# Moving the modulation's vector products behind late tiles, output weights and evacuations

## Chip, cores and metric

One core of a Trainium2 chip runs one launch of the kernel. The metric is device time in microseconds (us), the median of three runs. The engines are TensorE (PE, matrix products), VectorE (DVE), ScalarE (ACT), GpSimd (POOL, idle here) and SyncE (SP), which issues every DMA. Each takes its instructions in a fixed order, and waits by semaphores for the others.

## What is computed

One layer of a streaming encoder, in float32, for 1024 tokens of width 1024, cut to what matters here:

```python
mod = silu(c) @ ada_w + ada_b                     # 6 x 1024 values
shift1, scale1, gate1, shift2, scale2, gate2 = split(mod, 6)
h = rmsnorm(x, norm1_g) * (1 + scale1) + shift1
u_lx, u_ly, u_b, u_c, u_v = split(h @ w_in)       # 5 x 512 columns
y_lru = headwise_rmsnorm(gelu(u_ly) * rg_lru(conv4(u_lx)))
y_conv = headwise_rmsnorm(u_b * conv3(u_c * u_v))
x = x + gate1 * (concat(y_lru, y_conv) @ w_out)
h2 = rmsnorm(x, norm2_g) * (1 + scale2) + shift2
x = x + gate2 * (square(relu(h2 @ w_mlp1)) @ w_mlp2)
return rmsnorm(x, final_g)
```

## The kernel before

Activations lie transposed: 128 features on the partitions, tokens along the row, in two chunks of 512 tokens (`cc` 0 and 1), eight blocks of features (`n` or `k`). Every float32 operand of a large product is split into a high and a low part of type float32r (`split`, L98: an ACT copy L100, then a DVE subtraction L101), and a product is three matmuls (`mm3`, lines L105, L107, L109). The MLP behind it, from about 350 us on, uses seven products of half-size blocks in place of eight; the change does not touch it.

The order on each engine comes from a scheduler that places the program's instructions by their operands and its own estimates of time. Only `after(inst, prev)` adds an order by hand: `inst` is put behind `prev` on an engine, without a semaphore.

The stages around the change:

- Twenty column tiles of `w_in` (`nt`): 0 to 3 feed the recurrence, 4 to 7 its gelu, 8 to 19 the short convolution (b, c, v). Seven (`START`) come first, then thirteen (`LATE`, index `i` 0 to 12), whose weights are loaded and split by `load_late`. Each tile ends in a PSUM bank that `evac` empties by ACT and DVE.
- When a recurrent tile `n` has both parts, `lru_c(n)` runs the gates: two small products on PE, sigmoid, tanh, exp and square root on ACT, and on DVE the steps L450, L456, the scan L458 and L459, which multiplies by the gelu. `conv_v` and `conv_b` do the same for the convolution (L477, L481). Then `norm_out` squares, splits and sums over heads with two statistics matmuls by the block matrix `bones` (L409 with the high part, L410 with the low), and scales.
- `w_out` comes in eight blocks (`load_w(OS[n], wout[n])`). The output projection writes banks 0 to 5, then 0, 1, 2 again; `evac_out` (L571) empties a bank: L573 multiplies by gate1 and adds x, a DMA writes x to `x1d`, ACT squares (L575), L577 adds the squares. When all eight blocks of a chunk are in, `norm2` sums them over partitions with the row-sum matmul L703.

The modulation for the first norm is made early. The other 32 rows of `ada_w` (16 to 47, gate1 first, then scale2 and shift2 in turn, then gate2) are made by **vector products**: `gemv(idx)` (L207) loads 128 x 1024 of `ada_w` by SP into one of two buffers that `vraw` hands out in turn, and one DVE instruction, L210, multiplies it by silu(c) and sums along the row into a column of `mods`; one or two scalar instructions (L215, L216, L219) turn the column into the value used. `more_gemv(n)` (L223) takes the next n of the rows 16 to 39. Before, it is called once in each late tile but the first, twice among the output weights, and for the rest at the evacuations of chunk 0; the only order by hand is that a product comes behind `h_done`, the end of the first norm of chunk 1. So the scheduler may take a product as soon as its data is there.

Of the kernel before, what the change touches and what calls it, by code (L numbers as in the profile page):

```python
# [12 lines left out]
ALU = mybir.AluOpType  # L13
# [4 lines left out]
H = 512  # L18
# [17 lines left out]
def block_kernel(ctx, tc, xT, vec, adaT, winA, winB, gw, wout, w1, w2, outT):  # L36
# [5 lines left out]
    def sb(name, shape, dt=F32):  # L42
        return pool.tile(shape, dt, name=name, tag=name)
# [10 lines left out]
    G = sb("G", [P, 2, H])  # L54
# [14 lines left out]
    A, V, T, dma = nc.scalar.activation, nc.vector, nc.tensor, nc.sync.dma_start  # L69
# [5 lines left out]
    def fl(ap):  # L75
        return ap.rearrange("p a b -> p (a b)")
# [12 lines left out]
    def vraw():  # L89

        vraw_i[0] += 1
        return (raws[2], F[:, 16:18, :])[vraw_i[0] % 2]

    def kc(k):

        return slice(k % 4 * P, k % 4 * P + P)
# [15 lines left out]
    def rs_(i):  # L112
        return R[:, i, HI, :], R[:, i, LO, :]
# [14 lines left out]
    def after(inst, prev):  # L128

        tc.add_manual_dep(ins_of(inst), ins_of(prev).name, NOSYNC, reason="order")  # L130
        return inst
# [75 lines left out]
    def gemv(idx, r=None, cv=None):  # L207
        r = vraw() if r is None else r
        after(dma(r, adaT[idx].rearrange("p (a b) -> p a b", b=H)), last)
        g = V.scalar_tensor_tensor(fl(r), fl(r), 0.5, fl(cb) if cv is None else cv, op0=ALU.mult, op1=ALU.mult, accum_out=mods[:, idx : idx + 1])  # L210
        after(g, h_done)

    def mod_scale_shift(base, k, gcol):
        i = base + 2 * k
        V.tensor_scalar(md[:, i : i + 1], mods[:, i : i + 1], pre[:, i : i + 1], gcol, op0=ALU.add, op1=ALU.mult)  # L215
        V.tensor_scalar(md[:, i + 1 : i + 2], mods[:, i + 1 : i + 2], vt[:, V_ADAB + i + 1 : V_ADAB + i + 2], None, op0=ALU.add)  # L216

    def mod_gate(i):
        V.tensor_scalar(md[:, i : i + 1], mods[:, i : i + 1], vt[:, V_ADAB + i : V_ADAB + i + 1], None, op0=ALU.add)  # L219
# [3 lines left out]
    def more_gemv(n):  # L223
        for _ in range(n):
            if gq:
                i = gq.pop(0)
                gemv(i)
                if i < 24:
                    mod_gate(i)
                elif i % 2 == 1:  # L230
                    k = (i - 25) // 2
                    mod_scale_shift(24, k, vt[:, V_N2 + k : V_N2 + k + 1])
# [32 lines left out]
    with tc.manual_schedule(engines={ET.DVE, ET.Activation, ET.SP}):  # L265
# [9 lines left out]
        for k in range(KT):  # L275
            i = T.matmul(banks[k // 4][:, kc(k)], lhsT=sc[:, k : k + 1].broadcast_to([P, P]), rhs=ident, start=True, stop=True)
# [41 lines left out]
        for k in range(KT):  # L318
# [32 lines left out]
            for j in range(NS):  # L351
                i = mm3([(banks[j],) + rs_(2 * k)], *wk(16 + 2 * j, k), k == 0, k == KT - 1)
# [81 lines left out]
    def lru_c(n):  # L434
        for cc in range(NCH):
            XL, G, r, I, TN, M = lset(cc)
            ba, bx = aux(), aux()
            xp = rs_(16 + 2 * n + cc)
            split(xp, XL)
            mm3([(ba,) + xp], gwh[:, 0, n, :], gwl[:, 0, n, :], True, True)  # L440
            mm3([(bx,) + xp], gwh[:, 1, n, :], gwl[:, 1, n, :], True, True)
            TA(r, ba, AF.Sigmoid, bias=vt[:, V_GAB + n : V_GAB + n + 1])
            TA(I, bx, AF.Sigmoid, bias=vt[:, V_GXB + n : V_GXB + n + 1])
            V.tensor_tensor(I, I, XL, op=ALU.mult)
        for cc in range(NCH):
            XL, G, r, I, TN, M = lset(cc)
            TA(TN, r, AF.Tanh, scale=sp8[:, n : n + 1])
            TA(r, r, AF.Exp, scale=nsp8[:, n : n + 1])
            A(M, r, AF.Square)
            V.scalar_tensor_tensor(M, M, 1.0, TN, op0=ALU.add, op1=ALU.mult)  # L450
        for cc in range(NCH):
            XL, G, r, I, TN, M = lset(cc)
            TA(M, M, AF.Sqrt)
            if cc == 0:
                V.memset(M[:, 0:1], 1.0)
            V.tensor_tensor(I, I, M, op=ALU.mult)  # L456
            init = 0.0 if cc == 0 else lset(cc - 1)[4][:, H - 1 : H]
            V.tensor_tensor_scan(TN, r, I, init, op0=ALU.mult, op1=ALU.add)  # L458
            V.tensor_tensor(G, G, TN, op=ALU.mult)  # L459
            later.append(lambda cc=cc, G=G, M=M, I=I: norm_out(n, cc, G, M, I, aux(), n))  # L460

    def conv_c(n, cc, pc):
# [2 lines left out]
    def conv_v(n, cc, pv):  # L465
        CV, CC = E[:, 2 + cc, :], cset(cc)[0]
        w = lambda j: vt[:, V_SCW + 3 * n + j : V_SCW + 3 * n + j + 1]
        if cc == 0:
            V.memset(CV[:, 0:2], 0.0)
        else:  # L470
            V.tensor_copy(CV[:, 0:2], vh[:, n, :])
        V.tensor_tensor(CV[:, 2 : H + 2], pv, CC, op=ALU.mult)
        if cc + 1 < NCH:
            V.tensor_copy(vh[:, n, :], CV[:, H : H + 2])
        A(CC, CV[:, 2 : H + 2], AF.Identity, scale=w(2))
        for j in range(2):
            V.scalar_tensor_tensor(CC, CV[:, j : j + H], w(j), CC, op0=ALU.mult, op1=ALU.add)  # L477

    def conv_b(n, cc, pb):
        CV, (CC, SQ) = E[:, 2 + cc, :H], cset(cc)  # L480
        V.tensor_tensor(CC, CC, pb, op=ALU.mult)  # L481
        later.append(lambda: norm_out(4 + n, cc, CC, SQ, CV, aux(), 4 + n))

    def evac(nt, cc, bank):
# [19 lines left out]
    def load_w(slot, src):  # L504
        r = raw()
        dma(r, src.rearrange("p (a b) -> p a b", b=H))
        return split((R[:, slot : slot + 2, HI, :], R[:, slot : slot + 2, LO, :]), r)
# [37 lines left out]
    for i, nt in enumerate(LATE):  # L545
        load_late(i + 3)
        b0, b1 = bank(), bank()
        for k in range(KT):
            mm3([(b0,) + rs_(2 * k), (b1,) + rs_(2 * k + 1)], *wk(ring[i % 4], k), k == 0, k == KT - 1)
        evac(nt, 0, b0)  # L550
        evac(nt, 1, b1)
        if nt // 4 == 1:
            lru_c(nt % 4)
        flush()
        more_gemv(1 if i else 0)


    OS = [32, 34, 36, 0, 2, 4, 6, 8]
    for q in range(4):
        load_x(0, q)  # L560
    for n in range(KT):
        load_w(OS[n], wout[n])
        more_gemv(n % 4 // 3)

    def gate(base, n):
        return md[:, base + n : base + n + 1]
# [3 lines left out]

    def evac_out(n, cc, b, first, acc, sqt, cs=slice(0, H), add=True):  # L571
        x, acc, sqt = x1(cc, n)[:, cs], acc[:, cs], sqt[:, cs]
        V.scalar_tensor_tensor(x, b, gate(16, n), x, op0=ALU.mult, op1=ALU.add)  # L573
        dma(x1d[cc, :, n, cs], x)
        A(acc if first else sqt, x, AF.Square)  # L575
        if add and not first:
            V.tensor_tensor(acc, acc, sqt, op=ALU.add)  # L577
# [13 lines left out]
    for n in (6, 7):  # L591
        for k in range(KT):
            mm3([(banks[n - 6],) + y_(k, 0)], *wk(OS[n], k), k == 0, k == KT - 1)
        evac_out(n, 0, banks[n - 6], False, e4[0], e4[2 + n % 2])
        more_gemv(2)
    for q in range(4):
        load_x(1, q)
    more_gemv(48)
# [400 lines left out]
    for u in range(8, 16):  # L999
        v = u - 8  # L1000
        g, half = v // 2, v % 2
# [160 lines left out]
```

## Time and profile before

| | |
|---|---|
| median of 3 runs | 984.37 us (983.35 to 984.83) |
| profiled execution | 982.71 us |
| its span, first to last instruction | 980.8 us |
| PE busy | 963.6 us, 98%, granted clock 0.998 |
| DVE busy | 750.2 us, 76% |
| ACT busy | 536.2 us, 55% |
| DMA | 154.50 MB, 158 GB/s on average |

A profile shows one execution. Busy time of PE is modelled: a matmul that follows a wait is drawn longer, and one is drawn until it leaves the array, while the next has begun. Idle time before an instruction is shown in brackets with what ended it.

### The profile page before, as it was taken

How to read it: one execution, taken by the hardware profiler on the slowest of the kernel's cores; microseconds unless marked ns; L12 is line 12 of the kernel's file. 1: busy time of each engine (PE TensorE's matmuls, PEld its weight loads, DVE VectorE, ACT ScalarE, POOL GpSimd, SP SyncE). 2: the span in 40 equal slices, each digit the busy share in tenths (PEclk: the TensorE clock that was granted, in tenths of full speed). 3: DMA queues.
4: the chain of work that ended last, by engine and by line, in shares of the span. 5: the costliest groups of instructions: out<-in, count | busy, mean ns of one | idle time of the engine just before them, and what ended most of it. 6: DMA issues, size and time to landing. Idle time of an engine off the chain costs nothing.

```text
span 980.8 us, 11613 instructions
## 1 busy us (share of the span) xinstructions
PE 963.6 (98%) x4430; PEld 797.7 (81%) x4430; DVE 750.2 (76%) x1001; ACT 536.2 (55%) x719; POOL 0.2 (0%) x4
## 2 busy tenths in 40 slices
PE   8999999999999999999999999999999999999996
PEld 6878778777888998888888888887888888888885
DVE  7989999967445889876655555798599599589657
ACT  6778888775322577554454554683253243144444
POOL 0000000000000000000000000000000000000000
PEclk9999999999999999999999999999999999999999
DMA  8925245234132131765533525789456157144005
GB/s 312 346 101 181 91 138 196 99 109 172 65 108 97 49 114 57 263 233 187 182 130 127 215 93 188 255 274 348 151 171 216 65 168 239 65 150 172 1 1 171
DMA packets 53287, 154.50 MB, mean 158 GB/s; under 512 B 5104, under 2 KB 10736, under 8 KB 53232
## 3 DMA queue, kind: packets, MB, share of 16 engines
q1 hardware_dynamic: 53232, 153.77, 44.7%
q8 instruction: 34, 0.56, 0.2%
q14 instruction: 21, 0.17, 0.1%
HBM read 116.00 MB, written 37.75 MB: 157 GB/s over the span
## 4 chain that ended last, share of the span: by engine, by line
PE 82%; DVE 9%; ACT 4%; DMA 3%; issue 2%; DVEq 0%; SPq 0%; ACTq 0%
PE bank L105 27%; PE bank L109 27%; PE bank L107 27%; DVE R L101 2%; DMA F<-adaT 2%; DVE F L427 1%; ACT F L400 1%; DVE F L210 1%; DVE F L458 1%; ACT R L100 1%; DMA gh<-hidd 1%; ACT L400 1%; DMA E<-hidd 1%; DVE F L459 0%; PE bank L410 0%
## 5 line engine op out<-in xcount | busy, mean ns | idle before, releaser
L105 PE MATMUL bank<-R 128*128 128x512 f32 (+1 forms) x1416 | 521.5, 380 | 3.8 <-DVE lp L182 2.0
L107 PE MATMUL bank<-R 128*128 128x512 f32 (+1 forms) x1416 | 520.7, 379 | 0.0
L109 PE MATMUL bank<-R 128*128 128x512 f32 (+1 forms) x1416 | 517.6, 379 | 0.0
L105 PEld LDWEIGHTS bank<-R 128*128 128x128 f32 x1416 | 266.4, 188 | 57.0 <-ACT R L241 3.0
L109 PEld LDWEIGHTS bank<-R 128*128 128x128 f32 x1416 | 266.2, 188 | 50.5 <-DVE R L245 0.4
L107 PEld LDWEIGHTS bank<-R 128*128 128x128 f32 x1416 | 266.4, 188 | 49.8 <-issue 0.7
L100 ACT ACTIVATE R<-F 128x1024 fp32r<-128x1024 f32 (+1 forms) x175 | 165.6, 958 | 178.5 <-PE bank L109 118.9
L101 DVE TENSOR_TENSOR R<-F,R 128x1024 fp32r<-128x1024 f32 (+1 forms) x175 | 190.1, 1097 | 58.9 <-ACT R L100 58.6
L986 DVE SCALAR_TENSOR_TENSOR F<-bank,md,F 128x512 f32<-128x512 f32 (+1 forms) x120 | 84.8, 711 | 48.8 <-PE bank L109 47.7
L899 ACT ACTIVATE F<-bank 128x512 f32<-128x512 f32 x44 | 26.2, 596 | 48.8 <-PE bank L109 48.4
L100 ACT ACTIVATE R<-G 128x1024 fp32r<-128x1024 f32 x23 | 24.3, 1057 | 32.6 <-PE bank L109 22.1
L101 DVE TENSOR_TENSOR R<-G,R 128x1024 fp32r<-128x1024 f32 x23 | 28.1, 1220 | 13.3 <-ACT R L100 13.3
L100 ACT ACTIVATE R<-E 128x1024 fp32r<-128x1024 f32 x26 | 27.4, 1054 | 8.9 <-DMA E<-hidd 8.6
L101 DVE TENSOR_TENSOR R<-E,R 128x1024 fp32r<-128x1024 f32 x26 | 31.6, 1217 | 0.0
L210 DVE SCALAR_TENSOR_TENSOR F<-F 128x1024 f32<-128x1024 f32 x24 | 29.0, 1216 | 1.7 <-DMA F<-adaT 1.6
L575 ACT ACTIVATE E<-F 128x512 f32<-128x512 f32 (+1 forms) x21 | 11.1, 528 | 32.2 <-DVE F L573 30.2
L400 ACT ACT_TABLE_LOAD x22 | 28.2, 1283 | 0.4
L899 ACT ACTIVATE E<-bank 128x512 f32<-128x512 f32 x20 | 11.9, 595 | 23.4 <-PE bank L109 23.4
L573 DVE SCALAR_TENSOR_TENSOR F<-bank,md,F 128x512 f32<-128x512 f32 (+1 forms) x21 | 12.7, 620 | 15.5 <-PE bank L109 15.5
L914 ACT ACTIVATE F<-bank 128x512 f32<-128x512 f32 x16 | 9.5, 597 | 20.3 <-PE bank L109 19.0
L903 ACT ACTIVATE F<-F 128x1024 f32<-128x1024 f32 x18 | 18.9, 1050 | 2.8 <-DVE F L933 1.5
L904 ACT ACTIVATE F<-F 128x1024 f32<-128x1024 f32 x18 | 19.1, 1058 | 0.4
(198 smaller groups left out, 734.8 us busy)
## 6 DMA issues: line engine op xcount, KB each, us to landing
F<-w SPq DMA_DIRECT2D x51, 512.0 KB, 3.8
hidd<-F SPq DMA_DIRECT2D x47, 512.0 KB, 4.5
F<-adaT SPq DMA_DIRECT2D x44, 512.0 KB, 4.3
E<-hidd SPq DMA_DIRECT2D x26, 512.0 KB, 5.5
F<-xT SPq DMA_DIRECT2D x16, 512.0 KB, 5.8
F<-hidd SPq DMA_DIRECT2D x15, 512.0 KB, 4.8
gh<-hidd SPq DMA_DIRECT2D x15, 512.0 KB, 5.1
F<-winB SPq DMA_DIRECT2D x13, 512.0 KB, 3.3
```

The lines of the kernel that those rows point to most:

```text
L100: a = A(dst[0], src, AF.Copy)
L101: return a, V.tensor_tensor(dst[1], src, fp(dst[0]), op=ALU.subtract)
L105: i = [T.matmul(b, lhsT=wl, rhs=xh, start=start, stop=False, **kw) for b, xh, xl in outs]
L107: T.matmul(b, lhsT=wh, rhs=xh, start=False, stop=False, **kw)
L109: T.matmul(b, lhsT=wh, rhs=xl, start=False, stop=stop, **kw)
L210: g = V.scalar_tensor_tensor(fl(r), fl(r), 0.5, fl(cb) if cv is None else cv, op0=ALU.mult, op1=ALU.mult, accum_out=mods[:, idx : idx + 1])
L400: i = A(*args, **kw)
L573: V.scalar_tensor_tensor(x, b, gate(16, n), x, op0=ALU.mult, op1=ALU.add)
L899: A(t[:, q, :], bk2[q], AF.Copy)
L903: A(t, t, AF.Relu)
L904: A(t, t, AF.Square)
L986: done_by["bank"] = V.scalar_tensor_tensor(x1(cc, n)[:, cs], b, gate(40, n), x1(cc, n)[:, cs], op0=ALU.mult, op1=ALU.add)
```

## The change

A list `near` collects DVE instructions as the program is written out: the steps of a recurrent or convolution tile, the low split of a `wout` block, and the evacuation L573. A vector product is put behind the newest of them. `more_gemv` now takes none in the late tiles 0 to 7, two in each of 8 to 12, one behind each of the `wout` blocks 3 to 7, and one behind each evacuation of chunk 0; the rest (one) comes after.

```diff
--- before.py
+++ after.py
@@ -209,6 +209,11 @@
         after(dma(r, adaT[idx].rearrange("p (a b) -> p a b", b=H)), last)
         g = V.scalar_tensor_tensor(fl(r), fl(r), 0.5, fl(cb) if cv is None else cv, op0=ALU.mult, op1=ALU.mult, accum_out=mods[:, idx : idx + 1])
         after(g, h_done)
+        if near:
+            after(g, near[-1])
+
+
+    near = []
 
     def mod_scale_shift(base, k, gcol):
         i = base + 2 * k
@@ -456,7 +461,7 @@
             V.tensor_tensor(I, I, M, op=ALU.mult)
             init = 0.0 if cc == 0 else lset(cc - 1)[4][:, H - 1 : H]
             V.tensor_tensor_scan(TN, r, I, init, op0=ALU.mult, op1=ALU.add)
-            V.tensor_tensor(G, G, TN, op=ALU.mult)
+            near.append(V.tensor_tensor(G, G, TN, op=ALU.mult))
             later.append(lambda cc=cc, G=G, M=M, I=I: norm_out(n, cc, G, M, I, aux(), n))
 
     def conv_c(n, cc, pc):
@@ -474,11 +479,11 @@
             V.tensor_copy(vh[:, n, :], CV[:, H : H + 2])
         A(CC, CV[:, 2 : H + 2], AF.Identity, scale=w(2))
         for j in range(2):
-            V.scalar_tensor_tensor(CC, CV[:, j : j + H], w(j), CC, op0=ALU.mult, op1=ALU.add)
+            near.append(V.scalar_tensor_tensor(CC, CV[:, j : j + H], w(j), CC, op0=ALU.mult, op1=ALU.add))
 
     def conv_b(n, cc, pb):
         CV, (CC, SQ) = E[:, 2 + cc, :H], cset(cc)
-        V.tensor_tensor(CC, CC, pb, op=ALU.mult)
+        near.append(V.tensor_tensor(CC, CC, pb, op=ALU.mult))
         later.append(lambda: norm_out(4 + n, cc, CC, SQ, CV, aux(), 4 + n))
 
     def evac(nt, cc, bank):
@@ -552,15 +557,15 @@
         if nt // 4 == 1:
             lru_c(nt % 4)
         flush()
-        more_gemv(1 if i else 0)
+        more_gemv(2 if i > 7 else 0)
 
 
     OS = [32, 34, 36, 0, 2, 4, 6, 8]
     for q in range(4):
         load_x(0, q)
     for n in range(KT):
-        load_w(OS[n], wout[n])
-        more_gemv(n % 4 // 3)
+        near.append(load_w(OS[n], wout[n])[1])
+        more_gemv(1 if n > 2 else 0)
 
     def gate(base, n):
         return md[:, base + n : base + n + 1]
@@ -570,7 +575,7 @@
 
     def evac_out(n, cc, b, first, acc, sqt, cs=slice(0, H), add=True):
         x, acc, sqt = x1(cc, n)[:, cs], acc[:, cs], sqt[:, cs]
-        V.scalar_tensor_tensor(x, b, gate(16, n), x, op0=ALU.mult, op1=ALU.add)
+        near.append(V.scalar_tensor_tensor(x, b, gate(16, n), x, op0=ALU.mult, op1=ALU.add))
         dma(x1d[cc, :, n, cs], x)
         A(acc if first else sqt, x, AF.Square)
         if add and not first:
@@ -592,7 +597,7 @@
         for k in range(KT):
             mm3([(banks[n - 6],) + y_(k, 0)], *wk(OS[n], k), k == 0, k == KT - 1)
         evac_out(n, 0, banks[n - 6], False, e4[0], e4[2 + n % 2])
-        more_gemv(2)
+        more_gemv(1)
     for q in range(4):
         load_x(1, q)
     more_gemv(48)
```

**DVE, the end of the recurrence of tile n = 1** (F and E are working tiles, R holds split operands, lines from 212 on are 5 higher after the change). Before:

```order
L419 MEMSET E_65 128x3
L210 SCALAR_TENSOR_TENSOR F_64,mods_72<-F_64 128x1024
L455 MEMSET F_64 128x1
L456 TENSOR_TENSOR F_64<-F_64 128x512 x2
L427 SCALAR_TENSOR_TENSOR F_64<-E_65,vt_66,F_64 128x512
L458 SCALAR_TENSOR_TENSOR F_64<-F_64 128x512
L101 TENSOR_TENSOR R_63<-F_64,R_63 128x512
L459 TENSOR_TENSOR F_64<-F_64 128x512
L458 SCALAR_TENSOR_TENSOR F_64<-F_64 128x512
L101 TENSOR_TENSOR R_63<-F_64,R_63 128x512
L459 TENSOR_TENSOR F_64<-F_64 128x512
```

After:

```order
L432 SCALAR_TENSOR_TENSOR F_64<-E_65,vt_66,F_64 128x512
L455 SCALAR_TENSOR_TENSOR F_64<-F_64 128x512
L432 SCALAR_TENSOR_TENSOR F_64<-E_65,vt_66,F_64 128x512 x2
L460 MEMSET F_64 128x1
L461 TENSOR_TENSOR F_64<-F_64 128x512 x2
L463 SCALAR_TENSOR_TENSOR F_64<-F_64 128x512
L101 TENSOR_TENSOR R_63<-F_64,R_63 128x2x512
L464 TENSOR_TENSOR F_64<-F_64 128x512
L463 SCALAR_TENSOR_TENSOR F_64<-F_64 128x512
L101 TENSOR_TENSOR R_63<-F_64,R_63 128x512
L464 TENSOR_TENSOR F_64<-F_64 128x512
```

The product L210 ahead of the two steps L456 (now L461) is gone, and a weight split stands between the scan and L464. In PE's order the first statistics matmul of this tile stands 22 matmuls further ahead.

**DVE, the first evacuations of chunk 0** (bank0 to bank5 are the projection's banks, E the squares). Before:

```order
L648 TENSOR_TENSOR F_64<-F_64 128x1024
L573 SCALAR_TENSOR_TENSOR F_64<-bank0_80,md_73,F_64 128x512
L573 SCALAR_TENSOR_TENSOR F_64<-bank1_81,md_73,F_64 128x512
L573 SCALAR_TENSOR_TENSOR F_64<-bank2_82,md_73,F_64 128x512
L573 SCALAR_TENSOR_TENSOR F_64<-bank3_83,md_73,F_64 128x512
L577 TENSOR_TENSOR E_65<-E_65 128x512
L573 SCALAR_TENSOR_TENSOR F_64<-bank4_84,md_73,F_64 128x512
L577 TENSOR_TENSOR E_65<-E_65 128x512
L573 SCALAR_TENSOR_TENSOR F_64<-bank5_85,md_73,F_64 128x512
L577 TENSOR_TENSOR E_65<-E_65 128x512 x3
L573 SCALAR_TENSOR_TENSOR F_64<-bank0_80,md_73,F_64 128x512
L577 TENSOR_TENSOR E_65<-E_65 128x512
```

After:

```order
L210 SCALAR_TENSOR_TENSOR F_64,mods_72<-F_64 128x1024
L221 TENSOR_SCALAR md_73<-mods_72,vt_66 128x1
L578 SCALAR_TENSOR_TENSOR F_64<-bank0_80,md_73,F_64 128x512
L210 SCALAR_TENSOR_TENSOR F_64,mods_72<-F_64 128x1024
L578 SCALAR_TENSOR_TENSOR F_64<-bank1_81,md_73,F_64 128x512
L221 TENSOR_SCALAR md_73<-mods_72,vt_66 128x1
L210 SCALAR_TENSOR_TENSOR F_64,mods_72<-F_64 128x1024
L582 TENSOR_TENSOR E_65<-E_65 128x512
L578 SCALAR_TENSOR_TENSOR F_64<-bank2_82,md_73,F_64 128x512
L220 TENSOR_SCALAR md_73<-mods_72,pre_74,vt_66 128x1
L210 SCALAR_TENSOR_TENSOR F_64,mods_72<-F_64 128x1024
L582 TENSOR_TENSOR E_65<-E_65 128x512
```

A product stands behind each evacuation, and the adds of the squares come later; the row-sum matmul of PE comes three matmuls later in PE's order.

**SP, the same place** (x1d is written by an evacuation, adaT holds `ada_w`). Before:

```order
L636 DMA F_64<-w1 128x1024
L506 DMA F_64<-wout 128x1024
L147 DMA F_64<-xT 128x1024 x2
L506 DMA F_64<-wout 128x1024
L574 DMA x1d_89<-F_64 128x512 x11
L574 DMA x1d_89<-F_64 128x256 x6
```

After:

```order
L641 DMA F_64<-w1 128x1024
L511 DMA F_64<-wout 128x1024
L209 DMA F_64<-adaT 128x1024 x3
L579 DMA x1d_89<-F_64 128x512
L209 DMA F_64<-adaT 128x1024
L579 DMA x1d_89<-F_64 128x512
L209 DMA F_64<-adaT 128x1024
L579 DMA x1d_89<-F_64 128x512
L209 DMA F_64<-adaT 128x1024
```

The loads of the products now alternate with the writes of x1d, and a `wout` load has adaT loads on both sides.

## Rows read from the trace of the kernel before

**Rows 1.** Part 1 of the page: busy time and share of the span.

```profile
PE 963.6 (98%) x4430; PEld 797.7 (81%) x4430; DVE 750.2 (76%) x1001; ACT 536.2 (55%) x719; POOL 0.2 (0%) x4
```

**Rows 2.** Busy us by stretch: its length, each engine with records, clock, DMA.

```profile
78.00:222.00 144.00, 141.96 (x613) 113.28 (x612) 132.87 (x236) 117.91 (x171) 0.00 (x0) 1.00 0.40 135
120.00:142.00 22.00, 21.39 (x94) 17.34 (x93) 21.52 (x41) 18.22 (x27) 0.00 (x0) 1.00 0.44 151
240.00:260.00 20.00, 20.00 (x90) 16.57 (x89) 6.92 (x13) 4.11 (x7) 0.00 (x0) 1.00 0.08 29
294.00:314.00 20.00, 20.00 (x90) 16.57 (x89) 10.19 (x15) 5.08 (x8) 0.00 (x0) 1.00 0.28 105
```

**Rows 3.** Timeline of PE, 313 to 314 us: start, drawn us, engine, line.

```profile
313.23 0.39 PE L105 MATMUL bank<-R 128*128 128x512 f32 x1
...
313.91 0.59 PE L703 MATMUL bank<-E,ones 128*128 128x512 f32 x1
```

**Rows 4.** What PE waited for, 78 to 222 us: total, times, longest.

```profile
PE bank L409 <- ACT R L100: 1.3, 3, 0.6
PE bank L410 <- DVE R L101: 0.6, 2, 0.4
```

**Rows 5.** Groups of DVE by line and form, 60 to 300 us.

```profile
L210 DVE SCALAR_TENSOR_TENSOR F<-F 128x1024 f32<-128x1024 f32 x24 | 29.0, 1216 | 1.7 <-DMA F<-adaT 1.6
```

**Rows 6.** Timeline of DVE, 115 to 125 us.

```profile
116.18 0.20 DVE L219 TENSOR_SCALAR md<-mods,vt 128x1 f32<-128x1 f32 x1
116.31 1.21 DVE L210 SCALAR_TENSOR_TENSOR F<-F 128x1024 f32<-128x1024 f32 x1
...
119.03 1.23 DVE L210 SCALAR_TENSOR_TENSOR F<-F 128x1024 f32<-128x1024 f32 x1 [1.26 <-DMA F<-adaT]
120.18 0.08 DVE L210 DVE_READ_ACCUMULATOR F<-F 128x1 f32 x1
...
124.66 1.23 DVE L210 SCALAR_TENSOR_TENSOR F<-F 128x1024 f32<-128x1024 f32 x1
```

**Rows 7.** Timeline of DVE, 134 to 136 us.

```profile
134.20 1.22 DVE L210 SCALAR_TENSOR_TENSOR F<-F 128x1024 f32<-128x1024 f32 x1
...
135.35 0.68 DVE L456 TENSOR_TENSOR F<-F 128x512 f32<-128x512 f32 x1
```

**Rows 8.** Timeline of ACT, 133 to 134 us.

```profile
133.28 1.15 ACT L400 ACTIVATE F<-F 128x512 f32<-128x512 f32 x2
```

**Rows 9.** Busy us of L210 alone, last gate to first statistics matmul, n = 0 to 3.

```profile
84.00:103.00 19.00, 4.72 (x8) 1.00 0.55 178
123.00:140.00 17.00, 3.85 (x8) 1.00 0.47 156
159.00:175.00 16.00, 4.19 (x8) 1.00 0.46 164
202.00:219.00 17.00, 0.00 (x0) 1.00 0.27 95
```

**Rows 10.** Timeline of DVE, 294 to 298 us.

```profile
294.39 2.79 DVE L573 SCALAR_TENSOR_TENSOR F<-bank,md,F 128x512 f32<-128x512 f32 x4 [5.14 <-PE bank L109]
297.10 0.68 DVE L577 TENSOR_TENSOR E<-E 128x512 f32<-128x512 f32 x1
297.70 0.74 DVE L573 SCALAR_TENSOR_TENSOR F<-bank,md,F 128x512 f32<-128x512 f32 x1
```

**Rows 11.** DMA view: issues by line, KB each, median us to landing.

```profile
F<-adaT SPq DMA_DIRECT2D x44, 512.0 KB, 4.3
...
F<-wout SPq DMA_DIRECT2D x8, 512.0 KB, 3.3
```

**Rows 12.** Timeline of DVE, 340 to 342 us.

```profile
340.28 0.48 DVE L573 SCALAR_TENSOR_TENSOR F<-bank,md,F 128x256 f32<-128x256 f32 x1 [1.08 <-PE bank L109]
341.31 0.42 DVE L577 TENSOR_TENSOR E<-E 128x256 f32<-128x256 f32 x1 [0.54 <-ACT E L575]
```

**Rows 13.** Timeline of PE, 342.9 to 343 us.

```profile
342.96 0.38 PE L703 MATMUL bank<-E,ones 128*128 128x256 f32 x1
```

## The prediction, made before the change was run

> **What bounds the kernel now.** Read part 1 of the page first: TensorE (PE) is busy 98% of 980.8 us, VectorE (DVE) 76%, ScalarE (ACT) 55% [rows 1]. The change adds no arithmetic, so it can win only time in which PE does not run at its pace, and lose only by making PE wait. The second view, busy time by stretch, says where that is [rows 2]. From 78 to 222 us, where the 24 vector products now run, DVE is nearly full (21.52 of 22.00 us in 120 to 142) and PE idles 2.04 of 144.00 us; from 240 to 260 PE never idles and DVE is slack (6.92 of 20.00).
>
> Busy time hides part of the loss, because a matmul that follows a wait is drawn longer. So count: three matmuls take 0.68 us (313.23 to 313.91) [rows 3], 0.2267 each. The 613 records of 78 to 222 would take 139.0 us at that pace and took 144.0. **5.0 us is therefore the most this stretch can give back.** The waits that the profile names are 1.9 us, in five places, all before the two statistics matmuls L409 and L410 of a head-wise norm, on the ACT or DVE half of a split [rows 4].
>
> **The change, part by part.**
>
> *Products leave the recurrent tiles.* A product's main instruction is drawn with 1216 ns, 24 take 29.0 us [rows 5]; it holds DVE 1.15 us (119.03 to 120.18), and a scalar instruction behind it 0.13 (116.18 to 116.31) [rows 6]. What this costs a chain is seen at 134.20: a product runs, and L456, the first step of the recurrence, starts at 135.35 [rows 7], while ACT had finished both square roots at 134.43 [rows 8]. Without the product L456 could start 0.9 us sooner. But the scheduler has used this: it moves the statistics matmuls forward in PE's order as well. What counts is the distance from the last gate matmuls of a recurrent tile to its first statistics matmul. In PE's order it shrinks by 9, 7, 8 and 10 matmuls for the tiles n = 0 to 3, so the chain between has 2.0, 1.6, 1.8 and 2.3 us less. Out of that same chain products worth 4.72, 3.85, 4.19 and 0.00 us of DVE are taken [rows 9]. For n = 0 to 2 more is freed than is asked for, though part of it ran beside ACT and not in the chain; for n = 3 nothing is freed on DVE, so its wait stays. Bounds: 0 (each wait comes back) and 5.0. I take 2.0, the idle that the windows show [rows 2]: about what n = 0 to 2 lose, with the refill behind each wait, some 0.1 us, left in.
>
> *Products beside late tiles 8 to 12 and beside output weights.* Fifteen of the 24 products run here now, with their scalars about 15 x 1.3 = 20 us in the 72 us from 222 to 294, where DVE has 13 of 20 us spare (240 to 260) [rows 2]. Their DMAs share SP's queue with wout and x loads, and an adaT load that waits for its buffer holds what is behind it. Cover: before the first evacuation, at 294.39, DVE has done its splits and idles 5.14 us [rows 10]. So this costs nothing up to about 5 us of delay; with that cover gone, PE would wait for a wout split, and the delay beyond 5 us would count in full.
>
> *Products between the evacuations of chunk 0.* Here the cover is thin. DVE is busy 10.19 of 20.00 us from 294 to 314 [rows 2]; eight products (31 to 38) stand before the last add now. From the first evacuation to the add of n = 7: eight evacuations at 0.68 (2.79 for four, overlapped), seven adds at 0.60 (297.10 to 297.70) [rows 10], eight products at 1.15 and seven scalar instructions at 0.13 [rows 6] make 5.4 + 4.2 + 9.2 + 0.9 = 19.7 us. PE reaches the row-sum matmul L703, which needs that add, 313.91 - 294.39 = 19.5 us after the first evacuation [rows 3, 10], plus three matmuls that now stand ahead of it, 20.2. So DVE alone is just in time, with 0.5 us to spare.
>
> Then the loads. Two buffers serve the products, and the load for product k + 2 starts when product k has read its buffer, now also behind an x1d write on SP. In the trace the product of 119.03 leaves its buffer at 120.18, and the next one on that buffer runs at 124.66 [rows 6]: 5.63 us for two products, 2.8 each, against 19.7 / 8 = 2.5 that DVE needs anyhow. Six loads (33 to 38) late by 0.3 are 1.8 us, less 0.5 of cover: 1.3. With the 3.3 us that a wout load takes [rows 11], a pair would come round in 4.5, and nothing is late: 0. With 0.25 more for each, for SP's x1d issues, it is 0.55 x 6 - 0.5 = 2.8. Bounds 0 and 2.8; I take 1.2, from the row that has the products themselves.
>
> The Trainium skill, page "SBUF — State Buffer", section "The DMA setup-cost knee", puts a DMA at about 2 us plus its bytes over 436 GB/s. For 512 KB that is an estimate of 3.2 us, and by it no load would be late and the sum 1.2 us lower. The trace agrees for wout (3.3) and not for adaT (median 4.3) [rows 11]; the row decides.
>
> *Behind the row sum.* Norm 2 of chunk 0 shifts with PE's own wait. One sum for the MLP weights (L647) slides behind it, since its buffer now waits for the last product. The next row sum, at 342.96 [rows 13], has its last add done at 341.73, with 1.08 and 0.54 us of DVE idle just before [rows 12]: 1.2 us of cover plus these. Bounds 0 and 1.0 (a weight sum of 1.2 and the row sum's lateness, less that cover); I take 0.2.
>
> **Sum:** -2.0 + 1.2 + 0.2 = -0.6 us. The profiled execution took 982.71 us (its span is 980.8), so 982.1; the median of the three runs is 984.37, 1.66 above the profiled one, so 983.8. No change here means within 0.2%, 2.0 us, about what a measurement of this kernel can tell.
>
> **Rivals.**
>
> *Both halves go well (faster).* DVE was what held all four tiles, the waits vanish with most of the lost pace (5.0 less 1.5 for some fifteen refills at 0.1), and loads land in 3.3 us, so only the 0.2 remains: -3.3, or 981.1. For it: DVE is full exactly where PE waits [rows 2]. Against: ACT has 18.22 of 22.00 us there, and three of the five waits name ACT [rows 2, 4]. The skill's rule above would give this rival its second half.
>
> *The waits come back (no change).* The matmuls moved forward by as much as the chain did, so the gain is 0.4 and the row sum costs 1.2 + 0.2: +1.0, 985.4. For it: tile 3, which is asked for 2.3 us and gets none.
>
> *The row sum is late (slower).* Place: L703 behind the eight products. With 0.25 us more per load it is 2.8 us late, the second row sum 0.4, and the gain is 1.0: +2.2, 986.6. It decides the sign once the lateness exceeds the gain, and it can be measured once it exceeds the gain by 2.0. For it: the two buffers were short already at 124.66 [rows 6], with no x1d write between. Against: a wout load lands in 3.3 [rows 11].
>
> That the change does nothing is out: the printed order shows every product moved, 9 of them behind the first evacuation.
>
> **How the numbers follow.** Forecast 0.45, both go well 0.28, waits come back 0.12, row sum late 0.15. Faster by over 0.2%: 0.28 and 0.03 from the forecast's edge, 0.31. Slower: 0.15, 0.02 from the waits and 0.01 from the forecast's edge, 0.18. The rest, 0.51, is no change. The likeliest case alone spans 982.4 to 985.4 (gain 1 to 3, loss 0.6 to 2.0). The range for 8 in 10 reaches most of both outer cases, 981.4 to 986.6.
>
> **What would show it.** Right: no L210 between 86 and 200; PE idle from 78 to 222 below 1 us, and what is left at tile 3; DVE over 19 of 20 us in the 20 us behind the first evacuation; about 1 us of PE idle before the row sum, with DVE waiting for adaT just before. Wrong: no wait at the row sum, or one over 2.5 us; waits of the old size at the statistics matmuls; or any PE wait between 222 and 290, which would mean that the products hold up a bank or a wout split.

## The result: 0.7% slower, and the profile after

| | before | changed |
|---|---|---|
| median of 6 runs | 983.70 us (982.53 to 984.83) | 990.48 us (988.47 to 992.23) |
| ratio, 95% interval | | 1.0073 (1.0063 to 1.0084) |
| profiled execution | 982.71, span 980.8 | 992.23, span 990.3 |

The forecast was 983.8 us with a range of 981.4 to 986.6; the time lies above the range, and the change made the kernel slower instead of faster. In the changed kernel the lines behind the edit are numbered 5 higher (L703 is L708, L409 is L414, L573 is L578, L577 is L582); L210 kept its number.

Part 1 of the page, to be held against [rows 1]:

```profile
PE 968.0 (98%) x4430; PEld 799.7 (81%) x4430; DVE 752.9 (76%) x1001; ACT 537.1 (54%) x719; POOL 0.2 (0%) x4
```

Busy time by stretch, against [rows 2] (after the stretch its length, then each engine with its records, the clock, the DMA share and GB/s):

```profile
78.00:222.00 144.00, 141.90 (x612) 113.28 (x611) 106.86 (x168) 121.90 (x174) 0.00 (x0) 1.00 0.14 49
120.00:142.00 22.00, 21.40 (x93) 16.76 (x92) 16.18 (x26) 18.83 (x27) 0.00 (x0) 1.00 0.09 28
240.00:260.00 20.00, 20.00 (x90) 16.57 (x89) 12.30 (x25) 4.75 (x7) 0.00 (x0) 1.00 0.29 92
294.00:314.00 20.00, 20.00 (x90) 16.53 (x89) 15.69 (x29) 3.96 (x7) 0.00 (x0) 1.00 0.70 237
314.00:330.00 16.00, 12.92 (x43) 9.44 (x42) 13.79 (x21) 7.25 (x11) 0.00 (x0) 0.79 0.53 181
```

Two things stand here. DVE lost a fifth of its work between 78 and 222 us (132.87 to 106.86) and TensorE gained nothing by it: 141.90 us busy, 141.96 before. And from 314 to 330 TensorE has only 43 records in 16 us, at a mean clock of 0.79.

What TensorE waited for, from 78 to 222 us and, below the dots, from 310 to 330 (total, times, longest); the first two answer to [rows 4]:

```profile
PE bank L414 <- ACT R L100: 1.1, 2, 0.6
PE bank L415 <- DVE R L101: 0.9, 2, 0.7
...
PE bank L708 <- DVE E L582: 3.1, 1, 3.1
```

The timeline of TensorE at the row sum (start, drawn us, engine, line, what it waited for), against [rows 3]:

```profile
316.02 0.39 PE L109 MATMUL bank<-R 128*128 128x512 f32 x1
319.49 2.08 PE L708 MATMUL bank<-E,ones 128*128 128x512 f32 x2 [3.08 <-DVE E L582]
320.58 1.42 PE L105 MATMUL bank<-R 128*128 128x512 f32 x1
321.79 0.63 PE L107 MATMUL bank<-R 128*128 128x512 f32 x1
322.21 0.63 PE L109 MATMUL bank<-R 128*128 128x512 f32 x1
```

TensorE stands still for 3.1 us, and then its matmuls follow each other every 0.42 us (321.79 to 322.21) instead of every 0.2267 [rows 3]. That is the lower of the clock's two levels, 1.2 GHz in place of 2.4. The granted clock by stretch shows how long (length, PE with records, clock, DMA share, GB/s):

```profile
316.00:320.00 4.00, 0.92 (x3) 0.85 0.66 241
320.00:326.00 6.00, 6.00 (x14) 0.53 0.66 218
326.00:330.00 4.00, 4.00 (x20) 1.00 0.02 6
```

Six microseconds at 0.53 lose 0.47 x 6 = 2.8 us. "PE busy 6.00 of 6.00" hides this loss; the clock column and the 14 records show it.

Why the add is late is on DVE's timeline:

```profile
311.27 1.22 DVE L210 SCALAR_TENSOR_TENSOR F<-F 128x1024 f32<-128x1024 f32 x1 [0.38 <-DMA F<-adaT]
...
312.42 0.69 DVE L582 TENSOR_TENSOR E<-E 128x512 f32<-128x512 f32 x1
313.02 0.74 DVE L578 SCALAR_TENSOR_TENSOR F<-bank,md,F 128x512 f32<-128x512 f32 x1
314.23 1.23 DVE L210 SCALAR_TENSOR_TENSOR F<-F 128x1024 f32<-128x1024 f32 x1 [0.46 <-DMA F<-adaT]
...
317.60 1.23 DVE L210 SCALAR_TENSOR_TENSOR F<-F 128x1024 f32<-128x1024 f32 x1 [0.57 <-DMA F<-adaT]
...
318.75 0.69 DVE L582 TENSOR_TENSOR E<-E 128x512 f32<-128x512 f32 x1
```

The pattern is evacuation, product, add, and from the third product on a wait for its row of adaT before each. Two products on one buffer lie 6.33 us apart (311.27 and 317.60). The transfers in this stretch, 294 to 322 us (count, KB each, median us to landing), against [rows 11]:

```profile
F<-adaT SPq DMA_DIRECT2D x7, 512.0 KB, 5.0
x1d<-F SPq DMA_DIRECT2D x8, 256.0 KB, 4.1
```

To see where time is lost, compare the start of the same matmul, counted in TensorE's order, in the trace of before and in another. The lag grows as follows, in us; the second trace of the changed kernel is the last experiment below. The right columns are the kernels with four and three product buffers.

| stretch of the trace of before | changed | changed, second trace | four buffers | three buffers |
|---|---|---|---|---|
| start to 85 us | 1.00 | 1.53 | 0.43 | 0.90 |
| 85 to 237, recurrent tiles | 0.12 | 1.08 | -0.12 | -0.07 |
| 237 to 313, late tiles and output weights | 0.54 | 0.55 | 0.49 | 0.81 |
| 313 to 328, the row sum | 6.27 | 3.33 | 0.00 | 0.00 |
| 328 to 954 | 1.55 | -0.14 | -0.12 | -0.15 |

The first and the last line differ between two executions of one program; they are not read as the change.

### The profile page after: what moved, and what is told of

It reads as the page before. It is cut to its first block, busy times and chain, and to the rows that moved or that the text cites. A ratio compares the mean times of both kernels' runs of the same rounds, so it can differ in the third digit from the quotient of the medians.

```text
span 990.3 us, 11606 instructions
## 1 busy us (share of the span) xinstructions
PE 968.0 (98%) x4430; PEld 799.7 (81%) x4430; DVE 752.9 (76%) x1001; ACT 537.1 (54%) x719; POOL 0.2 (0%) x4
## 4 chain that ended last, share of the span: by engine, by line
PE 79%; ACT 8%; DVE 7%; DMA 5%; issue 1%; DVEq 0%; SPq 0%; ACTq 0%
PE bank L105 26%; PE bank L109 26%; PE bank L107 26%; DMA F<-adaT 2%; ACT R L100 2%; ACT F L405 2%; DVE R L101 1%; ACT L405 1%; DMA E<-hidd 1%; DMA F<-wout 1%; DVE F L210 1%; DVE F L463 1%; DMA F<-hidd 0%; DVE F L461 0%; PE bank L414 0%
## 5 line engine op out<-in xcount | busy, mean ns | idle before, releaser
L101 DVE TENSOR_TENSOR R<-F,R 128x1024 fp32r<-128x1024 f32 (+1 forms) x175 | 190.0, 1099 | 58.9 <-ACT R L100 58.8
L991 DVE SCALAR_TENSOR_TENSOR F<-bank,md,F 128x512 f32<-128x512 f32 (+1 forms) x120 | 85.0, 713 | 49.1 <-PE bank L109 47.7
L101 DVE TENSOR_TENSOR R<-G,R 128x1024 fp32r<-128x1024 f32 x23 | 28.1, 1222 | 12.6 <-ACT R L100 12.6
L101 DVE TENSOR_TENSOR R<-E,R 128x1024 fp32r<-128x1024 f32 x26 | 31.7, 1220 | 1.9 <-ACT R L100 1.9
L210 DVE SCALAR_TENSOR_TENSOR F<-F 128x1024 f32<-128x1024 f32 x24 | 28.9, 1221 | 3.7 <-DMA F<-adaT 3.7
L580 ACT ACTIVATE E<-F 128x512 f32<-128x512 f32 (+1 forms) x21 | 11.0, 526 | 31.4 <-DVE F L578 29.4
L904 ACT ACTIVATE E<-bank 128x512 f32<-128x512 f32 x20 | 11.9, 595 | 23.4 <-PE bank L109 23.4
L919 ACT ACTIVATE F<-bank 128x512 f32<-128x512 f32 x16 | 9.4, 596 | 19.8 <-PE bank L109 18.3
L432 DVE SCALAR_TENSOR_TENSOR F<-E,vt,F 128x512 f32<-128x512 f32 x24 | 17.9, 748 | 1.2 <-ACT F L430 1.1
```

What stands on the lines that cost most here:

```text
L101: return a, V.tensor_tensor(dst[1], src, fp(dst[0]), op=ALU.subtract)
L432: i = V.scalar_tensor_tensor(XL, U[:, j : j + H], w(j), XL, op0=ALU.mult, op1=ALU.add)
L904: A(t[:, q, :], bk2[q], AF.Copy)
L991: done_by["bank"] = V.scalar_tensor_tensor(x1(cc, n)[:, cs], b, gate(40, n), x1(cc, n)[:, cs], op0=ALU.mult, op1=ALU.add)
```

## The experiments

The theories that the expectations name: **1**, the row sum waits for the loads of the products between the evacuations, and the clock falls behind that wait, as a price of its own; **2**, the ties to late tiles and output weights cost the time; **3**, DVE's own work is what is late, not the loads; **4**, DVE's lateness is the whole price, and the slow matmuls hide a part of it; **5**, the gain from 78 to 222 us was there, but the scheduler had moved the statistics matmuls forward by as much.

### Loads, or DVE's own work?

**Four buffers.**

```diff
-        return (raws[2], F[:, 16:18, :])[vraw_i[0] % 2]
+        v = [raws[2], F[:, 16:18, :]]
+        if wide:
+            v += [F[:, 8:10, :], F[:, 10:12, :]]
+        return v[vraw_i[0] % len(v)]
...
-    for q in range(4):
+    for q in (2, 3, 0, 1):
         load_x(1, q)
```

`wide` is set ahead of the evacuations. The last pair loads last those pieces of x whose place the extra buffers take.

> The changed kernel, its DVE order kept but for a few one-column operations, where the products of the evacuations rotate over four buffers instead of two (two more from pieces that chunk 1 reads later). Theory 1, as loads: the products no longer wait for their rows of adaT; evacuation, product and add come to 2.7 us a piece, so the last add ends near 316 us, the row sum waits 0 to 0.8 us, the clock stays at 1.00, median 983.5 to 985. Theory 3 (DVE's own work is what is late, the loads only look so): the wait stays at 2 us or more and the median at 988 or more.

Measured: 984.13 us, ratio to before 1.0004 (0.9994 to 1.0013). TensorE waits for nothing at the row sum, its clock stays at 1.00. On DVE's timeline the eighth evacuation, the eighth product and the last add follow each other without a gap:

```profile
312.48 0.73 DVE L582 SCALAR_TENSOR_TENSOR F<-bank,md,F 128x512 f32<-128x512 f32 x1
313.14 1.21 DVE L214 SCALAR_TENSOR_TENSOR F<-F 128x1024 f32<-128x1024 f32 x1
314.28 0.08 DVE L214 DVE_READ_ACCUMULATOR F<-F 128x1 f32 x1
314.28 0.68 DVE L586 TENSOR_TENSOR E<-E 128x512 f32<-128x512 f32 x1
```

(In this kernel L210 is L214, L578 is L582, L582 is L586.) First evacuation at 295.19, last add done at 314.96: 19.8 us, where the prediction had summed 19.7 for DVE alone. The changed kernel needs 296.05 to 319.44, 23.4. All products and all ties are still there, and the loss at the row sum is gone: theory 3 falls. (The 0.5 us that is lost between 237 and 313 us stays, see the table.)

**Three buffers.** The same with `F[:, 8:10, :]` alone.

> The changed kernel with three product buffers behind the evacuations instead of two. Theory 1 by its rate (a load lands some 4.8 us after the product before it in its buffer has ended, the product takes 1.2 us, so two buffers give one product in 3.1 us and three one in 2.1 us, against 2.7 us of DVE's own work per output block): three buffers are as good as four, no product waits, row sum on time, clock 1.00, 983.5 to 985. If the loads are bound by what the DMA engines carry in that stretch and not by the turn of the buffers: waits of 1 us or more remain and 986 or more.

Measured: 984.01 us, 1.0008 (0.9997 to 1.0018). No product waits ahead of the last add, and the row sum is on time. The loads land no sooner (median 5.1 us in 294 to 322); it is the turn of two buffers, 5.0 us and a product of 1.2 in 6.2 or more, that was too slow, not the DMA engines.

**Products moved ahead of the evacuations.**

```diff
-        more_gemv(2 if i > 7 else 0)
+        more_gemv(3 if i > 7 else 0)
...
-        more_gemv(1 if n > 2 else 0)
+        more_gemv(2 if n == 0 else 1)
...
-        more_gemv(1)
+        pass
```

The last pair is behind the evacuations, in both loops.

> The changed kernel with its ties, but three products a late tile (8 to 12) in place of two, two at output block 0 and one at each later block, and none issued by the evacuation loops: the schedule then leaves 2 of the products between evacuations instead of 9. Theory 1 (the row sum waits 3.1 us for the ninefold line of product loads between the evacuations, and the half clock that follows that wait takes about as much again): no wait above 0.5 us at the row sum, granted clock 1.00 behind it, median 983.0 to 984.8, the kernel before. Theory 2 (the ties to late tiles and to output weights cost the time, wherever the last products stand): still 987 or more.

Measured: 987.50 us (985.34 to 989.65), 1.0041 (1.0025 to 1.0058). The time is the one that theory 2 named (987 or more), by half a microsecond; at the row sum it is as theory 1 has it, with no wait and the clock at 1.00. TensorE's waits from 222 to 330 us are now

```profile
PE bank L105 <- DVE F L486: 0.8, 1, 0.8
PE bank L105 <- DVE R L101: 0.5, 1, 0.5
PE bank L414 <- ACT R L100: 0.4, 1, 0.4
```

L101 is the DVE half of a weight split and L486 the last step of a convolution: with more products among them, DVE brings output weights and banks too late. Between 237 and 313 us this trace loses 2.3 us, the changed kernel 0.54. So there is a price for products in this stretch too; in the changed kernel theory 2 holds for a small part. The trace is of an execution of 986.27 us; three of the six took 988.7 to 989.7, and what these lost no trace shows.

**Ties at the evacuations alone**, on the kernel before:

```diff
+        if near:
+            after(g, near[-1])
...
-        more_gemv(n % 4 // 3)
+        more_gemv(1 if n > 4 else 0)
...
-        V.scalar_tensor_tensor(x, b, gate(16, n), x, op0=ALU.mult, op1=ALU.add)
+        near.append(V.scalar_tensor_tensor(x, b, gate(16, n), x, op0=ALU.mult, op1=ALU.add))
...
-        more_gemv(2)
+        more_gemv(1)
```

(The first piece is in `gemv`, the last behind evacuations 6 and 7.)

> The kernel before with its early products left untied (12 in the late tiles, 3 at output blocks 5 to 7) and only the nine behind the evacuations tied to them. Theory 1: a wait of 2.5 to 3.5 us at the row sum, half the granted clock for some 6 us behind it, and 989.5 to 991.5. Theory 2: the row sum comes within 1 us of where it was before and the median is 985.5 or less.

Measured: 987.64 us, 1.0043 (1.0027 to 1.0060). The row sum waits 2.3 us and the clock is at 0.72 from 320 to 326; the lag grows by 4.18 us there. The place is the one that theory 1 named. Eight products stand ahead of the last add, as in the changed kernel, but four of them wait for their rows of adaT (2.5 us in all) instead of six (3.05). The traced execution, 990.52 us, is in theory 1's range; the other three took 987.1 to 988.1, and what their clock did at the row sum no trace shows. The traced one also lost 2.3 us between 85 and 237 us, so its time is not the price of the row sum alone.

### Does the clock fall belong to the wait?

**A wait without loads.** Vector operations of a product's size hold up the last add; the order of TensorE is that of before, held by order dependencies.

```diff
+            if (n, cc) == (7, 0):
+                for _ in range(5):
+                    e = after(V.scalar_tensor_tensor(fl(R[:, 10]), fl(cb), 0.5, fl(cb), op0=ALU.mult, op1=ALU.mult), e)
-            V.tensor_tensor(acc, acc, sqt, op=ALU.add)
+            i = V.tensor_tensor(acc, acc, sqt, op=ALU.add)
+            if (n, cc) == (7, 0):
+                after(i, e)
```

`e` is the evacuation; the other kernel has 4 in place of 5. In both, the row sum is L709 and the add L580.

> The kernel before, TensorE's order word for word, with four vector operations of a product's size (1.2 us each, on data that nobody reads) ahead of DVE's last add for the row sum; no loads in it. They use up the 3 us that the row sum had to spare: wait of 0.6 to 1.0 us at the row sum, last add near 314.7 us. Theory 1: too short for the clock to fall, median 984 to 984.8. If any wait there costs as much again: 985.5 or more.

> The same with five of them: a wait of 2.2 to 3.0 us at the row sum, from DVE alone. Theory 1: the granted clock halves behind it as in the changed kernel, 2 to 3 us more, median 987.5 to 989.5. Theory 4 or a cause of the half clock in the loads: clock at 1.00 behind the row sum, and 986 to 986.6.

Measured with four: 985.40 us, 1.0016 (1.0007 to 1.0025). With five: 987.59 us, 1.0037 (1.0028 to 1.0046). TensorE's timeline with five:

```profile
313.66 0.39 PE L109 MATMUL bank<-R 128*128 128x512 f32 x1
316.76 2.08 PE L709 MATMUL bank<-E,ones 128*128 128x512 f32 x2 [2.71 <-DVE E L580]
...
319.06 0.63 PE L107 MATMUL bank<-R 128*128 128x512 f32 x1
319.48 0.63 PE L109 MATMUL bank<-R 128*128 128x512 f32 x1
...
320.20 0.39 PE L107 MATMUL bank<-R 128*128 128x512 f32 x1
```

and with four:

```profile
316.71 1.13 PE L709 MATMUL bank<-E,ones 128*128 128x512 f32 x2 [0.92 <-DVE E L580]
317.27 0.79 PE L105 MATMUL bank<-R 128*128 128x512 f32 x1
317.91 0.39 PE L107 MATMUL bank<-R 128*128 128x512 f32 x1
318.14 0.40 PE L109 MATMUL bank<-R 128*128 128x512 f32 x1
```

A wait of 0.9 us costs 1.18 us of lag and leaves the clock alone. A wait of 2.7 us costs 4.53, and the matmuls behind it run at the lower level until about 320 us, though no product and no load of one is near. (One 512 KB weight load lands there, with four operations as with five; with four the clock stays at 1.00.) So the fall needs no product loads; it came behind the longer wait. Each of the two has one trace.

**The wait filled**: 14 matmuls into a bank that nobody reads stand between the last matmul ahead of the row sum and the row sum.

```diff
+    for i in range(14):
+        fill.append(T.matmul(banks[7], lhsT=wk(OS[7], 0)[0], rhs=y_(7, 1)[0], start=True, stop=True))
+        after(fill[-1], (fill[:-1] or tile)[-1])
     norm2(0, full, banks[6])
```

The row sum's matmul is ordered behind all of `fill`, and `tile` holds the matmuls of the output tile ahead.

> The changed kernel with 14 matmuls more (3.2 us at full clock), into a PSUM bank that nobody reads, tied between the last matmul ahead of the row sum and the row sum. The loads and the last add stay as late as they are. Theory 1: TensorE is busy where it waited, the matmuls behind the row sum keep their 0.227 us, and the median falls by the half clock alone, about 3 us, to 986.5 to 988. If the half clock does not come from the wait: spacing still 0.43 us behind the row sum, and 990 or more.

Measured: 990.27 us, 1.0076 (1.0055 to 1.0096). The clock is 1.00 behind the row sum, and yet nothing is won: the scheduler had put the first addition on the hidden layer's weights ahead of the row sum's scaling on DVE, which then waited 4.0 us for those weights, and TensorE waited 2.1 us at the second row sum. So once more with that addition held back:

```diff
-        V.tensor_tensor(s1, comp[u, 21], comp[u, 22], op=ALU.add)
+        i = V.tensor_tensor(s1, comp[u, 21], comp[u, 22], op=ALU.add)
+        if u == 0:
+            after(i, scaled[3])
```

`scaled[3]` is the last scaling by the row sum; the operation behind this one is tied in the same way.

> The changed kernel with the 14 matmuls in the wait at the row sum, as in the run before, and now with the first additions on the weights of the hidden layer held behind the row sum's own scaling on DVE, as the changed kernel has them (in the run before they had moved ahead of it and DVE stood 4.0 us for a weight load). Theory 1 (the half clock follows the wait and is a price of its own): full clock behind the row sum, no new wait at the second row sum above 0.5 us, 986.5 to 988 us. Theory 4 (DVE's lateness is the whole price, and the slow matmuls only hide a part of it): the second row sum waits 2 us or more and the median stays at 989.5 or more.

Measured: 989.79 us, 1.0053 (1.0038 to 1.0069). TensorE's timeline (L786 is the 14 matmuls, L713 the row sum):

```profile
315.44 3.33 PE L786 MATMUL bank<-R 128*128 128x512 f32 x14
319.33 1.12 PE L713 MATMUL bank<-E,ones 128*128 128x512 f32 x2 [0.56 <-DVE E L582]
...
320.52 0.40 PE L107 MATMUL bank<-R 128*128 128x512 f32 x1
320.76 0.40 PE L109 MATMUL bank<-R 128*128 128x512 f32 x1
```

The add is as late as in the changed kernel, TensorE is busy meanwhile, and the clock does not fall. One trace does not prove that filling prevents the fall, since the last run of this part shows a wait without one; but seven of the eight timed executions of the two filled kernels have a mean granted clock of 0.996 or more, against three of ten of the changed kernel. The lag grows by 4.01 us at the row sum, which now stands three matmuls (0.68 us) further ahead, and by 0.81 at the second row sum: 4.82 in all, between the two traces of the changed kernel. The time is in theory 4's range (989.5 or more), but its sign is missing: the second row sum waits 0.6 us and not 2. The slow matmuls do not hide that part either, for the last run has none and loses nothing there (0.00 from 328 to 352 us). ScalarE's order differs:

```profile
322.35 0.63 ACT L580 ACTIVATE E<-F 128x512 f32<-128x512 f32 x1 [4.64 <-DVE F L578]
322.88 0.67 ACT L121 ACTIVATE E<-bank,epsc 128x512 f32<-128x512 f32 x1
```

L121 reads the row sum from its bank. Here, and in the first filled kernel, it stands behind a square L580 that waits for a late evacuation; in the changed kernel it stands ahead of that square (321.60 and 322.86). That this order is what makes the second row sum late was not tested alone.

**The row sum one output tile later.** `norm2(0, ..)` and what follows stand behind the next `out_tile`.

> The changed kernel with the row sum of chunk 0 and what follows it written behind the next output tile, so that TensorE has 24 matmuls more (5.4 us) ahead of it; products, ties and loads as they are. Theory 1: TensorE works where it waited: no wait at the row sum, full clock, and 984 to 985.5 unless the second row sum, whose chain on DVE starts 2.3 us later than in the changed kernel, takes over. Theory 4: the second row sum waits 2 us or more and the median is 987 or more.

Measured: 992.56 us, 1.0085 (1.0066 to 1.0103), no better than the change. The row sum waits for nothing, but DVE's order changed as in the first filled kernel. A line of DVE's timeline,

```profile
325.02 1.23 DVE L652 TENSOR_TENSOR F<-F 128x1024 f32<-128x1024 f32 x1 [3.63 <-DMA F<-w]
```

and what TensorE waits for from 300 to 360 us, now at the second row sum:

```profile
PE bank L708 <- DVE E L582: 4.9, 1, 4.9
```

The weights are late because their buffer carries the last product, which ends at 320.52; the load that DVE waits for starts at 320.64 and lands at 325.00. Moving the matmul that waits did not help here, where the chain behind it was as late; whether it would with DVE's order held was not tried.

**The changed kernel again**, unaltered.

> The changed kernel once more, unaltered, for a second trace. Theory 1: again a wait of 2.8 to 3.4 us and 2.5 to 3.3 us of half clock at the row sum, 989.5 to 991; what its first trace lost beside that, 1.0 us in the first 30 us and 1.5 us between 650 and 690 us, is of single executions and need not come back. If these belong to the change, both are there again.

Measured: 989.01 us, 1.0062 (1.0039 to 1.0085). TensorE's timeline:

```profile
317.52 0.39 PE L109 MATMUL bank<-R 128*128 128x512 f32 x1
320.96 1.13 PE L708 MATMUL bank<-E,ones 128*128 128x512 f32 x2 [3.05 <-DVE E L582]
321.53 0.80 PE L105 MATMUL bank<-R 128*128 128x512 f32 x1
322.16 0.40 PE L107 MATMUL bank<-R 128*128 128x512 f32 x1
322.40 0.40 PE L109 MATMUL bank<-R 128*128 128x512 f32 x1
```

The same wait, and this time the clock stays up: the row sum costs 3.33 us of lag instead of 6.27. So the wait is paid in both traces, the slow stretch in one of them. The timed executions fit that: of ten, the five with a mean granted clock of 0.992 or 0.993 took 989.1 to 992.2 us, the five with 0.994 to 0.996 took 987.5 to 989.8. (That clock is a mean over the whole execution, so this is a fit and no proof.)

### The gain that did not come

The first statistics matmul of tile n = 1, in the changed kernel and, below the dots, before:

```profile
137.21 0.50 PE L414 MATMUL bank<-R,bones 128*128 128x512 f32 x1 [0.60 <-ACT R L100]
...
141.06 0.50 PE L409 MATMUL bank<-R,bones 128*128 128x512 f32 x1 [0.61 <-ACT R L100]
```

It waits as long as it did, and stands 22 places further ahead in TensorE's order. Less the 1.0 us by which this trace runs behind, it starts 4.85 us sooner, 21 matmuls of 0.2267.

**Statistics matmuls held back**, once on the kernel with four buffers and once on the kernel before. A statistics matmul of a tile is ordered behind a later matmul of a late tile (i, k):

```diff
+    HOLD = {(0, 0): [(0, 0, 1)], (2, 5): [(1, 0, 0)], (2, 6): [(1, 1, 0)], (5, 0): [(2, 0, 0)],
+            (8, 5): [(3, 0, 0)], (8, 6): [(3, 0, 1)], (10, 4): [(6, 0, 0)]}
...
+            for s, cc, h in HOLD.get((i, k), ()):
+                after(stats[s, cc][h], m)
```

This is the table with four buffers; the kernel before has five such entries.

> The changed kernel with the four product buffers (its row sum then waits for nothing), and seven of its statistics matmuls held back in TensorE's order behind a later matmul of a late tile: they stand 5 to 20 places later than in the changed kernel. Theory 5 (the gain of 2.0 us that the prediction booked for 78 to 222 us was there, in DVE and ACT, but the scheduler had moved the statistics matmuls forward by as much as their operands came sooner, so that TensorE waited as before): the idle time of TensorE between 78 and 222 us falls from 2.1 us to 0.8 us or less, and the median comes 1.0 to 1.8 us below that of the four buffers alone, to 981.8 to 983.2 us. If those waits come from something else than the place in the order: idle 1.5 us or more, and 983.7 us or more.

> The kernel before, products as they are, with five statistics matmuls held back in the same way (most then stand 4 to 12 places later). Theory 5: TensorE's idle time between 78 and 222 us falls from 2.0 us to 1.2 us or less, median 982.3 to 983.3 us, without any tie on the products. If the products are what makes TensorE wait there: idle stays at 1.8 us or more, and 983.5 us or more.

Measured: 984.89 us, 1.0018 (1.0008 to 1.0028), with four buffers; 983.59 us, 1.0001 (0.9992 to 1.0010), on the kernel before. What TensorE waited for from 78 to 222 us, with four buffers (L420 and L421 are the statistics matmuls):

```profile
PE bank L421 <- DVE R L105: 1.4, 3, 0.7
PE bank L420 <- ACT R L104: 0.7, 2, 0.4
```

and on the kernel before (L411):

```profile
PE bank L411 <- ACT R L100: 3.3, 4, 1.1
```

The matmuls stood later, the scheduler ordered DVE and ACT anew around them, and the waits were back, 2.1 and 3.3 us. Theory 5 is half borne out. Waits of this size stay whatever the order: 1.9 us in before, 2.0 in the changed kernel with a fifth of DVE's work gone, 2.1 and 3.3 here. Why they stay is argued from the places above, not shown by a run. That holding the matmuls back in this way wins the time is refuted. What it would take to win it stays open. Nor is the sum of named waits the time lost: with 3.3 us of them the second kernel lags the one before by only 0.03 us between 85 and 237 us.

No kernel run here is faster than the one before; four or three buffers bring the change back to within what the runs can tell from it.

## Why the prediction was wrong

- **"I take 2.0" for the waits at the statistics matmuls: failed.** 0 was its lower bound, and nothing was gained: between 85 and 237 us the lag does not shrink but grows, by 0.12 us in one trace and 1.08 in the other. In tile n = 1 the matmul moved forward by 22 places, and its operand came 21 matmuls sooner (shown above). The prediction had set freed DVE time [rows 9] against the shortened distance and called the surplus a gain. But freed time on DVE is not freed time in the chain, and the distance had been set by the same scheduler from the same chain. The rival "the waits come back" had this right.
- **"Six loads late by 0.3 ... I take 1.2": failed, and together with the first it decides the result.** The mechanism was right, the size was not: the wait is 3.1 us, above the upper bound of 2.8, and costs 3.33 us of lag where the clock stays up. The pace of 5.63 us for two products [rows 6] came from a stretch in which the DMA engines were 0.44 busy [rows 2]; behind the evacuations they are 0.70 busy with the x1d writes among the loads, adaT lands in 5.0 (median) instead of the 4.3 of the whole trace [rows 11], and a pair takes 6.3. The six waits that DVE's timeline names ahead of the last add come to 3.05 us. By the prediction's own sum either miss alone would have left the time within the range (985.8 and 985.9 us); the two together give 987.9, outside it. Bounds on a load must come from a stretch as crowded as the one it moves to.
- **Missing: what TensorE's clock does behind a wait.** No term and no rival had it. It is 2.9 us (6.27 - 3.33) in the first trace, nothing in the second. The Trainium skill, page "TensorE: Matmul & The Clock Gate", section "What's actually happening", says that the clock has two levels, set by how busy TensorE was of late, and that the point at which it changes differs from run to run. The traces agree: 0.53 in one and 1.00 in the other, behind the same wait of 3.1 us.
- **"DVE alone is just in time": right**, and closely: 19.7 us summed, 19.8 measured with four buffers.
- **"This costs nothing up to about 5 us of delay" for the products beside the output weights: wrong by half a microsecond.** TensorE waits 0.4 us for a weight split near 278 us and loses 0.54 from 237 to 313. The cover taken, DVE's idle time just before the first evacuation [rows 10], lies behind the need for that weight. With more products there the loss became 2.3 us.
- **"I take 0.2" behind the row sum: 0.00** (7.93 us of lag at 328 us and at 352).
- Of the marks named ahead, "no L210 between 86 and 200" holds; "PE idle from 78 to 222 below 1 us" does not (2.10); "DVE over 19 of 20 us" does not (17.51 from 296.05 to 316.05, the 20 us behind the first evacuation), because DVE waited for rows of adaT in that time; and all three signs against the forecast came: a row-sum wait over 2.5 us, waits of the old size at the statistics matmuls, and a wait near 278 us.
- The sum by measured terms: row sum 3.3, output weights 0.5, recurrent tiles 0.1 to 1.1, and 0 to 2.9 for the clock, 3.9 to 7.8 us; the two comparisons give 6.8 (990.48 - 983.70) and 5.6 (989.01 - 983.46). The rival "the row sum is late" had the place and the cause, and priced it at 2.8 with a gain of 1.0 that did not exist.

## What to carry to other kernels

Work that is spread between the steps of a chain needs loads that come round as fast as the chain: compare (landing + use) / buffers with the chain's own step, 6.2 / 2 = 3.1 against 2.4 to 2.7 us here, and take the landing time from a stretch that is as crowded. A wait of TensorE of two to three microseconds may cost nearly as much again in clock (2.3 us cost 4.2 of lag, 2.7 cost 4.5, 3.1 cost 6.3 once and 3.3 once), so price it twice at the upper end and read the clock column, since busy time hides it. Where a scheduler sets the order, do not book time freed on an engine as time won: here the matmuls moved forward and their waits came back.

## What was not expected of the hardware

- Behind one wait of 3.1 us the granted clock fell to its lower level for some six microseconds in one execution (0.53 from 320 to 326) and not in another (1.00). Behind 2.7 and 2.3 us it fell, behind 0.9 it did not.
- The same 256 KB writes of x1d landed in 2.0 us (median, 294 to 322 us, in the kernel before and in the one with five stand-in vector operations, both without product loads there) and in 4.1 with product loads beside them; those took 5.0 for 512 KB. By the Trainium skill, page "SBUF — State Buffer", section "The DMA setup-cost knee", such a load is estimated at 3.2 us; the traces differ here and decide.
